# A routed-expert encoder block on one core: down sums in groups of 128 columns, weight slots returned one by one, and filler products on TensorE

## The chip, the cores and the metric

The kernel runs on one core of one Trainium2 chip. The metric is the device time of one execution in microseconds, shown as the median of several runs. The names of the engines are those of the profile: PE is TensorE (PEld its weight loads), DVE is VectorE, ACT is ScalarE, POOL is GpSimd, SP is SyncE, which here only issues DMA transfers.

## What is computed

One layer of an encoder on 256 tokens of 2,048 channels, all in float32. The reference, cut to what matters here:

```
mod = silu(c) @ W_ada + b_ada                     # 2048 x 12288: shift, scale, gate, twice
h   = rmsnorm(x, g_pre_mix) * (1 + sc1) + sh1
y   = hybrid_mixer(h, ...)                        # w_in (2048 x 10752), two branches, w_branch_a/b, w_out
x   = x + gt1 * rmsnorm(y, g_post_mix)
h   = rmsnorm(x, g_pre_ffn) * (1 + sc2) + sh2
aff = softmax(h @ w_router)                       # 256 tokens x 16 experts
top_aff, top_idx = top_k(aff.T, 32)               # each expert picks its 32 tokens
for each expert e:                                # FF = 1024
    xe = h[top_idx[e]]
    ye = (silu(xe @ w_gate[e]) * (xe @ w_up[e])) @ w_down[e]
    y[top_idx[e]] += top_aff[e] * ye
x   = x + gt2 * rmsnorm(y, g_post_ffn)
```

## The kernel before

**Tiles and slots.** Every weight matrix is laid out ahead of time as tiles of 128 partitions x 2,048 float32, 1 MB each, and read once from HBM: 96 tiles of `w_ada`, 84 of `w_in`, 8 + 8 of the branch projections, 16 of `w_out`, and for each of the 16 experts 16 tiles of gate and up columns (`w_gu`) and 8 of the down matrix (`w_dn`). SBUF has 27 slots of that size (`Mem`, a first-in first-out list). `take()` (lines 155 to 163) gets a slot and issues one transfer on SP's queue; if the slot is still being read by an engine, SP waits there, and all later transfers behind it. The order of the tiles, `stream`, is fixed ahead: first the mixer's program `prog` (lines 231 to 272), then expert after expert.

**The mixer.** Each tile of a projection is split into a high and a low part (`split`, lines 427 to 440: ACT copies at line 436, DVE subtracts at line 437), and `prod` (lines 442 to 466) does three TensorE products for each pair of parts. The parts live in a ring of `NHL = 6` of the 27 slots (`Ring`, lines 107 to 123), which come back to the common list only when the mixer's program is through (`hring.close()`, line 896). The merged branch results, MH and ML, take two slots each (each of them holds two of the four k-steps of the last projection); they too are returned at the very end (line 856). A `w_ada` tile ("A", "B" items) is no TensorE work but one DVE instruction (line 402). The constants in lines 35 to 38 say how many such tiles are mixed in where: BL for the late `w_in` projections (30 items with 12 tiles, then 14 with 14), BD for the branch projections and the last projection (16 items with 8 tiles, then the 14 of 16 that follow with 14).

**From the mixer to the first expert** (lines 899 to 1047). DVE and ACT finish the normalised residual X2 (`rsqrt`, lines 217 to 228, is a logarithm and an exponential on ACT with a Newton step on DVE). TensorE turns X2 and multiplies it by the router's matrix, a softmax follows, TensorE turns the affinities (line 967), DVE selects the 32 largest of each expert in four rounds (lines 971 to 981), TensorE turns the marks back (line 984), and `gather_first` (lines 1014 to 1046) builds the first expert's inputs in four groups of 128 columns: `rows(i)` gathers with one-hot products, `turn_rows(i)` turns them and DVE scales them. Two groups are gathered ahead of the first expert tile.

**The experts** (lines 1063 to 1163). For each of the 16 tiles k, four products go to four column strips of the array (`tile_position=(0, 32 * j)`), 512 columns each; then the tile's slot is returned. After the sixteenth, SiLU and the product `he`. The down matrix is done in four chunks of 512 output columns: `down_wide` (line 1141) sums two tiles into four strips that each hold a part of the contraction, and `combine_wide` (line 1152) has two TensorE products with `stw` (the affinities at the tokens' places, repeated for the four strips), which add the strips and scatter to 2 x 128 tokens; DVE adds the result to ACC (line 1160).

**The last expert and the output** (lines 1165 to 1228). Here the down matrix goes by nine steps (`STEPS`: seven of 256 columns, two of 128, the last tile in two transfers): `down(i)`, `combine(i - 1)`, then `squares(i - 2)` for the final norm (ACT; DVE for the last two), and `gain3(i - 2)`, the product with the post-norm gain on DVE (one step on GpSimd). Then the squares are reduced (line 1209), `rsqrt` with two late `gain3` in its shadow, and the output is formed and stored.

The order on an engine is that of the program text, unless `after(engine, f)` pins an instruction to come behind the latest one of its engine; on DVE, the whole order of the last expert is pinned from `mark` on (`finish_deps`). The lines of the order around the change:

```
STEPS = [(256 * i, 256) for i in range(7)] + [(1792, 128), (1920, 128)]   # line 35
BL = [(30, 12), (14, 14)]                                                # 37
BD = [(16, 8), (14, 14)]                                                 # 38
hring.put(hl)                                                            # 466, at the end of prod
if c == 3: mem.put(*MH, *ML)                                             # 855-856, only at q == 3
rows(0); rows(1); turn_rows(0)                                           # 1036-1038
```

## Time and profile before

| what | value |
|---|---|
| median of three runs | 1692.03 us (1691.38 to 1692.73) |
| the profiled execution | 1690.94 us, its span 1689.2 us |
| instructions | 19531 |
| mean granted TensorE clock | 0.911 of full speed |
| busy: PE, DVE, ACT, POOL | 1412.3, 769.1, 544.5, 1.6 us |
| HBM read, mean rate over the span | 630.04 MB, 374 GB/s |

Times in the trace count from the start of the span, in microseconds. The ends of matmuls are modelled, so a busy PE is not PE at its peak; a share of busy time is an average over stages that have different limits, so it has to be read stage by stage. A row of the timeline gives start, busy time, engine, line of the kernel, operation, output and inputs, how many instructions it stands for, and in brackets how long the engine had been idle before it and on what. The profile counts a float32 product as two instructions, each with its own weight load.

### The profile page before, as it was taken

To read this page: it belongs to the slowest core of one execution; us is meant where nothing else is said; L and a number is where in the kernel's file an instruction comes from. 1 tells how busy PE (TensorE), PEld (TensorE's weight loads), DVE (VectorE), ACT (ScalarE), POOL (GpSimd) and SP (SyncE) were. 2 spreads that over 40 slices of the span, in tenths; PEclk is the share of its full clock that TensorE was granted. 3 is DMA by queue.
4 is the path that set the end of the run, shared out by engine and by line. 5 is a ranking of instruction groups with operands and counts; after the bars stand their busy time and mean duration, and the time that the engine had idled before them with its cause. 6 is when DMAs were issued, how large, how long until landed. Compare 5 with 4: busy or idle time off the path is not lost.

```text
span 1689.2 us, 19531 instructions
## 1 busy us (share of the span) xinstructions
PE 1412.3 (84%) x7982; PEld 787.6 (47%) x7982; DVE 769.1 (46%) x1017; ACT 544.5 (32%) x793; POOL 1.6 (0%) x5
## 2 busy tenths in 40 slices
PE   4999999999999999988877776776776677677677
PEld 3999997787888888862211111111111111111113
DVE  8788879989878799742111111110111111111013
ACT  6577777765575434431100000000000000000013
POOL 0000000000000000000000000000000000000000
PEclk7999999999999999998998888797878979788798
DMA  9999975665778879989999999999999999999996
GB/s 386 420 421 375 356 324 223 254 233 198 293 277 341 348 280 377 421 355 420 421 421 420 421 421 421 421 420 421 421 422 421 421 422 421 421 421 421 422 421 279
DMA packets 88505, 633.41 MB, mean 375 GB/s; under 512 B 10080, under 2 KB 10464, under 8 KB 11744
## 3 DMA queue, kind: packets, MB, share of 16 engines
q1 hardware_dynamic: 88128, 631.39, 91.8%
q8 instruction: 62, 1.02, 0.2%
q10 hardware_dynamic: 288, 0.79, 0.1%
q14 instruction: 27, 0.22, 0.0%
HBM read 630.04 MB, written 2.10 MB: 374 GB/s over the span
## 4 chain that ended last, share of the span: by engine, by line
PE 48%; DMA 45%; DVE 3%; ACT 2%; issue 1%; SPq 0%; ACTq 0%; DVEq 0%
PE PS L180 46%; DMA w<-in_w_gu_dram 32%; DMA w<-in_w_dn_dram 12%; DMA w<-in_w_in_dram 1%; DVE hl L437 1%; DMA w<-in_w_ada_dram 1%; ACT ew L1150 0%; DVE w L402 0%; PE PS L917 0%; PE PS L1092 0%; PE PS L688 0%; DVE F L510 0%; ACT hl L436 0%; ACT ew L1089 0%; PE PS L770 0%
## 5 line engine op out<-in xcount | busy, mean ns | idle before, releaser
L180 PE MATMUL PS<-w,rt 128*32 128x512 f32 x2048 | 336.2, 727 | 155.8 <-DMA w<-in_w_gu_dram 154.9
L437 DVE TENSOR_TENSOR hl<-w,hl 128x1024 fp32r<-128x1024 f32 x232 | 278.0, 1220 | 87.2 <-ACT hl L436 86.4
L180 PE MATMUL PS<-hl,hl 128*128 128x256 f32 (+1 forms) x928 | 309.1, 334 | 0.0
L436 ACT CAST hl<-w 128x1024 fp32r<-128x1024 f32 x232 | 237.8, 1048 | 151.7 <-PE PS L180 142.9
L180 PE MATMUL PS<-hl,hh 128*128 128x512 f32 x832 | 269.8, 399 | 0.7 <-ACT hl L436 0.6
L180 PEld LDWEIGHTS PS<-w,rt 128*32 128x32 f32 x2048 | 52.3, 117 | 388.8 <-DMA w<-in_w_gu_dram 338.7
L402 DVE SCALAR_TENSOR_TENSOR w<-w,crow 128x2048 f32<-128x2048 f32 x96 | 218.8, 2284 | 3.7 <-DMA w<-in_w_ada_dram 3.5
L180 PE MATMUL PS<-hh,hl 128*128 128x256 f32 x1024 | 186.7, 285 | 9.3 <-ACT hh L420 9.3
L180 PEld LDWEIGHTS PS<-hl,hl 128*128 128x128 f32 x928 | 177.5, 191 | 16.3 <-issue 1.0
L1160 DVE TENSOR_TENSOR acc<-acc,PS 128x1024 f32<-128x1024 f32 x56 | 68.4, 1221 | 244.3 <-PE PS L180 244.3
L180 PE MATMUL PS<-ew,rt 128*128 128x512 f32 (+2 forms) x276 | 138.9, 629 | 45.1 <-ACT ew L1150 45.1
L180 PEld LDWEIGHTS PS<-hl,hh 128*128 128x128 f32 x832 | 155.4, 188 | 33.5 <-ACT hl L436 1.0
L180 PEld LDWEIGHTS PS<-hh,hl 128*128 128x128 f32 x1024 | 161.5, 194 | 9.6 <-ACT hh L420 9.5
L180 PE MATMUL PS<-w,ew 128*32 128x512 f32 (+2 forms) x1104 | 145.9, 636 | 19.7 <-DVE ew L1098 15.4
L1098 DVE TENSOR_TENSOR ew<-ew,PS 128x256 f32<-128x256 f32 x16 | 6.7, 421 | 241.0 <-ACT ew L1097 241.0
L180 PEld LDWEIGHTS PS<-ew,rt 128*128 128x128 f32 x276 | 49.4, 200 | 141.0 <-ACT ew L1150 105.6
L1150 ACT COPY ew<-PS 128x512 f32<-128x512 f32 x60 | 35.1, 585 | 237.1 <-PE PS L180 237.1
L1089 ACT COPY ew<-PS 128x512 f32<-128x512 f32 x16 | 9.4, 585 | 237.1 <-PE PS L180 237.1
L180 PEld LDWEIGHTS PS<-w,ew 128*32 128x32 f32 x1104 | 29.0, 118 | 118.5 <-issue 68.9
L180 PE MATMUL PS<-hl,mh 128*128 128x512 f32 x256 | 80.1, 393 | 0.0
L1053 DVE TENSOR_SCALAR rt<-ct,rt 128x128 f32<-128x128 f32 x32 | 9.6, 343 | 147.6 <-PE PS L1057 147.6
L1059 ACT COPY rt<-PS 128x256 f32<-128x256 f32 x16 | 6.0, 372 | 191.5 <-PE PS L1057 191.5
(252 smaller groups left out, 1111.1 us busy)
## 6 DMA issues: line engine op xcount, KB each, us to landing
w<-in_w_gu_dram SPq DMA_DIRECT2D x256, 1024.0 KB, 19.8
w<-in_w_dn_dram SPq DMA_DIRECT2D x127, 1024.0 KB, 19.8
w<-in_w_ada_dram SPq DMA_DIRECT2D x96, 1024.0 KB, 8.9
w<-in_w_in_dram SPq DMA_DIRECT2D x84, 1024.0 KB, 7.2
w<-in_w_out_dram SPq DMA_DIRECT2D x16, 1024.0 KB, 14.7
w<-in_w_a_dram SPq DMA_DIRECT2D x8, 1024.0 KB, 6.8
w<-in_w_b_dram SPq DMA_DIRECT2D x8, 1024.0 KB, 8.2
x<-in_x_dram SPq DMA_DIRECT2D x4, 1024.0 KB, 12.2
```

The source lines that it names most:

```text
L180: E.matmul(o, l, r, start=start, stop=stop, skip_group_check=True, **kw)
L402: V.scalar_tensor_tensor(t, t, 1.0, CR, ALU.mult, ALU.mult, accum_out=MOD[:, p, k:k + 1])
L436: S.copy(hl[:, 0, :], w)
L437: V.tensor_tensor(hl[:, 1, :], w, hl[:, 0, :].bitcast(F32), ALU.subtract)
L1053: V.tensor_scalar(rp[:, tt], io[:, None, :].to_broadcast([128, 4, 32]), pm3[:, tt, e:e + 1], aff[:, tt, e:e + 1], ALU.is_equal, ALU.mult)
L1059: S.copy(stw, b[:, :256])
L1089: S.copy(gu, b)
L1098: V.tensor_tensor(he, sl_, b3[:, :, 64:128], ALU.mult)
L1150: S.copy(EW[:, 2, :], b)
L1160: V.tensor_tensor(a, a, p3, ALU.add)
```

## The change

It has five parts.

1. **Slots and order of the mixer.** `Ring.put` gets the number of parts still to come (`todo`) and hands a slot back to the common list as soon as the ring's free slots are enough for them. MH and ML are returned in halves, at the second and the fourth k-step of the last projection. Four `w_ada` tiles are moved from the last projection to earlier ones: two to the late `w_in` projections, two to the branch projections.
2. **Fillers.** `warm(n, ...)` issues n float32 products of the identity with itself, whose result nobody reads: 11 behind the mixer's last product, 6 behind the router's sums, 20 behind the turn of the affinities.
3. **The path to the first expert.** `rsqrt` may be one ACT function (`Abs_reciprocal_sqrt`), used for the mixer's and the final norm; the squares of the residual are placed otherwise between ACT and DVE; the softmax works on both halves at once; `gather_first` gathers one group, not two, ahead of the first tile, and goes on with one half step between tiles.
4. **Down sums.** In all experts each chunk of 512 columns is done in four groups of 128: `down_quarters` puts group j, over the whole contraction, into strip j (16 products of 128 columns a tile), and `combine_quarters` scatters it with products of 32 rows (`tile_position=(32 * j, 0)`), eight a chunk, of 128 columns. ACT's copy has 128 columns, not 512. The combination of chunk c - 1 stands behind the products of chunk c.
5. **The last expert.** Three chunks of 512, then one step of 256 and two of 128. The gain of chunk 2 is half on GpSimd, half on DVE, that of the 256 columns on GpSimd; the layout of the last expert's tiles follows.

```diff
-STEPS = [(256 * i, 256) for i in range(7)] + [(1792, 128), (1920, 128)]
+WIDE = [(512 * i, 512) for i in range(4)]
+STEPS = WIDE[:3] + [(1536, 256), (1792, 128), (1920, 128)]
 BE = [2, 2, 2, 10]
-BL = [(30, 12), (14, 14)]
-BD = [(16, 8), (14, 14)]
+BL = [(30, 14), (14, 14)]
+BD = [(16, 10), (14, 10)]
...
-    def put(self, t):
-        self.slots.append(self.mem.slot.pop(id(t))[0])
+    def put(self, t, todo):
+
+        if todo <= len(self.slots):
+            self.mem.put(t)
+        else:
+            self.slots.append(self.mem.slot.pop(id(t))[0])
...
+        if direct:
+            S.activation(r, ss, AF.Abs_reciprocal_sqrt, scale=1.0 / D, bias=epsc)
+        else:
+            S.activation(l, ss, AF.Ln, scale=1.0 / D, bias=epsc)
+            S.activation(r, l, AF.Exp, scale=-0.5)
...
+    nsplit = [sum(it[0] in ("W", "YA", "YB", "O") for it in prog)]
...
-            hring.put(hl)
+            hring.put(hl, 2 * nsplit[0])
...
-                if c == 3:
-                    mem.put(*MH, *ML)
+            if c == 3 and q % 2:
+                mem.put(MH[q // 2], ML[q // 2])
...
+    def warm(n, o):
+
+        for _ in range(n):
+            after(mybir.EngineType.PE, lambda: mm(o, ident, ident, True, True))
+
+    warm(11, PS[:, 3072:3200])
...
+    warm(6, PS[:, 0:128])
     rm, rd = tiny(2), tiny(2)
     V.tensor_reduce(rm, l3, AX.X, ALU.max)
-    V.tensor_scalar(rm, rm, -1.0, None, ALU.mult)
+    V.tensor_tensor(l3, l3, rm[:, :, None].to_broadcast([128, NT, 16]), ALU.subtract)
...
+    warm(20, PS[:, 0:128])
...
         rows(0)
-        rows(1)
         turn_rows(0)
         yield xe
         for i in range(1, 4):
-            if i < 3:
-                after(mybir.EngineType.PE, lambda: rows(i + 1))
+            after(mybir.EngineType.PE, lambda: rows(i))
+            yield
             after(mybir.EngineType.PE, lambda: turn_rows(i))
             yield
...
+        def down_quarters(i):
+
+            b = bank()
+            for h in range(2):
+                w = take()
+                for kq in range(4):
+                    for j in range(4):
+                        mm(b[32 * j:32 * j + 32, :128], he[:, kq, 32 * h:32 * h + 32],
+                           w[:, 512 * kq + 128 * j:512 * kq + 128 * j + 128], h == 0 and kq == 0,
+                           h == 1 and kq == 3, tile_position=(0, 32 * j))
+                mem.put(w)
+            S.copy(sums(i), b[:, :128])
+
+        def combine_quarters(i):
+
+            ps = PS[:, :2048].rearrange("p (j r t c) -> p t j r c", j=4, r=2, t=2)[:, :, :, i % 2, :]
+            for tt in range(NT):
+                for j in range(4):
+                    mm(ps[:, tt, j, :], stw[32 * j:32 * j + 32, 128 * tt:128 * tt + 128],
+                       sums(i)[32 * j:32 * j + 32, :], True, True, tile_position=(32 * j, 0))
+            a = acc(i).rearrange("p t (j c) -> p t j c", j=4)
...
+                V.tensor_tensor(a, a, ps, ALU.add)
...
-            for c in range(4):
-                down_wide(c)
-                combine_wide(c)
+            for c in range(5):
+                if c < 4:
+                    down_quarters(c)
+                if c:
+                    after(mybir.EngineType.PE, lambda: combine_quarters(c - 1))
             continue
...
+        for i in range(3):
+            down_quarters(i)
+            if i:
                 after(mybir.EngineType.PE, lambda: combine(i - 1))
-            if 1 < i < ns:
-                squares(i - 2)
-                if i < ns - 1:
-                    gain3(i - 2)
-        gain3(ns - 3, nc.gpsimd)
-        squares(ns - 1)
+                squares(i - 1)
+                gain3(i - 1)
+        w = take()
+        after(mybir.EngineType.PE, lambda: combine(2))
+        after(mybir.EngineType.PE, lambda: down(3, w))
+        mem.put(w)
+        squares(2)
+        gain3(2, nc.gpsimd, slice(0, 1))
+        gain3(2, V, slice(1, 2))
...
+        squares(5)
+
+        nc.gpsimd.tensor_copy(tiny(1), sf8[:, 1, 5:6])
+        after(mybir.EngineType.Pool, lambda: gain3(3, nc.gpsimd))
...
-    r3 = rsqrt(sf, 2, lambda: (gain3(7), gain3(8)))
+    r3 = rsqrt(sf, 2, lambda: (gain3(4), gain3(5)), True)
```

The first place in the order is TensorE's between the router and the first tiles of the first expert (ct: the sum over strips of the router's products; rt: router's scratch; ident: turns and fillers; x: the residual, gathered from; w: expert tiles; line 180 is the common product helper, 185 after the change). Before:

```order
L180 MATMUL PS<-ct,rt_5864 128x16 x2
L967 MATMUL PS<-ident,rt_5864 16x128 x2
L984 MATMUL PS<-ident,rt_5864 128x16 x2
L180 MATMUL PS<-x_726_5593,rt_5864 32x128 x4
L180 MATMUL PS<-x_727_5595,rt_5864 32x128 x4
L180 MATMUL PS<-x_726_5593,rt_5864 32x128 x4
L180 MATMUL PS<-x_727_5595,rt_5864 32x128 x4
L1031 MATMUL PS<-ident,rt_5864 128x128
L180 MATMUL PS<-w_5996,rt_5864 32x512 x4
L180 MATMUL PS<-x_726_5593,rt_5864 32x128 x4
L180 MATMUL PS<-x_727_5595,rt_5864 32x128 x4
```

With the change:

```order
L185 MATMUL PS<-ct,rt_5875 128x16 x2
L185 MATMUL PS<-ident 128x128 x6
L988 MATMUL PS<-ident,rt_5875 16x128 x2
L185 MATMUL PS<-ident 128x128 x20
L1006 MATMUL PS<-ident,rt_5875 128x16 x2
L185 MATMUL PS<-x_728_5596,rt_5875 32x128 x4
L185 MATMUL PS<-x_729_5598,rt_5875 32x128 x4
L1053 MATMUL PS<-ident,rt_5875 128x128
L185 MATMUL PS<-w_6023,rt_5875 32x512 x4
L185 MATMUL PS<-x_728_5596,rt_5875 32x128 x4
L185 MATMUL PS<-x_729_5598,rt_5875 32x128 x4
L185 MATMUL PS<-w_6038,rt_5875 32x512 x4
```

Six and twenty fillers stand between, one gather group (eight rows of x as two times four) stands ahead of the first tile and not two, and each turn comes a tile later than its group.

The second place is TensorE's order in the last expert, to the last products with the sums, before from behind the fifth of the nine steps on, with the change from behind the fourth down tile on (w: down tiles, the last one in two halves; ew: the sums and `he`; rt: holds `stw`). Before:

```order
L180 MATMUL PS<-ew_6059,rt_5864 128x256 x2
L180 MATMUL PS<-w_9061,ew_6059 32x256 x8
L180 MATMUL PS<-ew_6059,rt_5864 128x256 x2
L180 MATMUL PS<-w_9078,ew_6059 32x256 x8
L180 MATMUL PS<-ew_6059,rt_5864 128x256 x2
L180 MATMUL PS<-w_9095,ew_6059 32x128 x8
L180 MATMUL PS<-ew_6059,rt_5864 128x256 x2
L180 MATMUL PS<-w_9095,ew_6059 32x128 x8
L180 MATMUL PS<-ew_6059,rt_5864 128x128 x4
```

With the change:

```order
L185 MATMUL PS<-ew_6095,rt_5875 128x128 x3
L185 MATMUL PS<-w_10911,ew_6095 32x128 x16
L185 MATMUL PS<-ew_6095,rt_5875 128x128 x5
L185 MATMUL PS<-w_10929,ew_6095 32x128 x16
L185 MATMUL PS<-ew_6095,rt_5875 128x128 x10
L185 MATMUL PS<-w_10960,ew_6095 32x256 x8
L185 MATMUL PS<-w_10984,ew_6095 32x128 x8
L185 MATMUL PS<-ew_6095,rt_5875 128x256 x2
L185 MATMUL PS<-w_10984,ew_6095 32x128 x8
L185 MATMUL PS<-ew_6095,rt_5875 128x128 x4
```

Nine steps of which each is followed by the combination of the one before it have become three chunks and three small steps; in these rows the sixth down tile is the fourth one, the combination of chunk 1 stands around it, and that of chunk 2 behind it.

The third place is VectorE's order there (acc: the sums over all experts, in two halves; G: the gain; line 1209, after the change 1248, is the reduction of the squares). Before:

```order
L1126 TENSOR_TENSOR acc_6150<-acc_6150,PS 128x2x256
L1139 TENSOR_TENSOR acc_6149<-acc_6149,G_1487_8861 128x2x256
L1126 TENSOR_TENSOR acc_6150<-acc_6150,PS 128x2x256
L1139 TENSOR_TENSOR acc_6150<-acc_6150,G_1487_8861 128x2x256
L1126 TENSOR_TENSOR acc_6150<-acc_6150,PS 128x2x256
L1139 TENSOR_TENSOR acc_6150<-acc_6150,G_1487_8861 128x2x256
L1126 TENSOR_TENSOR acc_6150<-acc_6150,PS 128x2x128
L1133 SCALAR_TENSOR_TENSOR rt_5864,small<-acc_6150 128x128
L1126 TENSOR_TENSOR acc_6150<-acc_6150,PS 128x2x128
L1133 SCALAR_TENSOR_TENSOR rt_5864,small<-acc_6150 128x128
L1209 TENSOR_REDUCE small<-small 128x2
```

With the change:

```order
L1161 TENSOR_TENSOR acc_6185<-acc_6185,PS 128x2x512
L1194 TENSOR_TENSOR acc_6185<-acc_6185,G_1493_10701 128x2x512
L1161 TENSOR_TENSOR acc_6185<-acc_6185,PS 128x2x512
L1194 TENSOR_TENSOR acc_6185<-acc_6185,G_1493_10701 128x2x512
L1161 TENSOR_TENSOR acc_6186<-acc_6186,PS 128x2x512
L1194 TENSOR_TENSOR acc_6186<-acc_6186,G_1493_10701 128x512
L1179 TENSOR_TENSOR acc_6186<-acc_6186,PS 128x2x256
L1179 TENSOR_TENSOR acc_6186<-acc_6186,PS 128x2x128
L1187 SCALAR_TENSOR_TENSOR rt_5875,small<-acc_6186 128x128
L1179 TENSOR_TENSOR acc_6186<-acc_6186,PS 128x2x128
L1187 SCALAR_TENSOR_TENSOR rt_5875,small<-acc_6186 128x128
L1248 TENSOR_REDUCE small<-small 128x2
```

The adds (lines 1126; 1161 and 1179) and the gain products (1139; 1194) alternate in both; those of 256 columns have become ones of 512, and the gain of half of chunk 2 stands between its add and the add of the 256 columns.

## Rows read from the trace of the kernel before

**Rows 1.** The page, the chain of work that ended last: shares of the span by engine.

```profile
PE 48%; DMA 45%; DVE 3%; ACT 2%; issue 1%; SPq 0%; ACTq 0%; DVEq 0%
```

**Rows 2.** Windows over the span: start and end in us, length; busy us and count of PE, PEld, DVE, ACT, POOL; granted TensorE clock, share of the DMA engines, GB/s.

```profile
300.00:400.00 100.00, 98.79 (x519) 80.04 (x518) 92.38 (x136) 65.32 (x90) 0.00 (x0) 1.00 0.55 205
...
600.00:650.00 50.00, 50.00 (x231) 41.56 (x231) 48.56 (x54) 20.50 (x22) 0.00 (x0) 1.00 0.84 326
...
750.00:800.00 50.00, 37.81 (x319) 14.34 (x312) 17.50 (x60) 11.57 (x28) 0.00 (x0) 0.86 1.01 420
...
1600.00:1650.00 50.00, 38.40 (x198) 8.77 (x190) 6.27 (x6) 5.06 (x9) 0.00 (x0) 0.87 1.01 421
```

**Rows 3.** The timeline of SP's queue from 735 to 800 us: start, length, and the number of transfers issued in the row.

```profile
742.76 1.28 SPq L161 DMA_DIRECT2D w<-in_w_gu_dram  x3
744.08 10.72 SPq L161 DMA_DIRECT2D w<-in_w_dn_dram  x8
769.61 27.97 SPq L161 DMA_DIRECT2D w<-in_w_gu_dram  x16
```

**Rows 4.** Windows of 2 us, with the columns of group 2.

```profile
740.00:742.00 2.00, 2.00 (x11) 1.65 (x10) 0.00 (x0) 0.00 (x0) 0.00 (x0) 1.00 0.00 0
...
760.00:762.00 2.00, 0.00 (x0) 0.00 (x0) 1.86 (x7) 0.00 (x0) 0.00 (x0) 0.50 1.00 418
...
768.00:770.00 2.00, 2.00 (x24) 0.79 (x16) 0.00 (x0) 0.00 (x0) 0.00 (x0) 0.50 1.00 418
```

**Rows 5.** Transfers issued in three narrow windows: from 742.7 to 742.9 us (the issue of 742.76), from 754.4 to 754.6 (the last of the eight down tiles, at 754.47) and from 769.5 to 769.8 (the one at 769.61). The last number is the time from issue to landing in us.

```profile
w<-in_w_gu_dram SPq DMA_DIRECT2D x1, 1024.0 KB, 4.7
...
w<-in_w_dn_dram SPq DMA_DIRECT2D x1, 1024.0 KB, 19.2
...
w<-in_w_gu_dram SPq DMA_DIRECT2D x1, 1024.0 KB, 6.6
```

**Rows 6.** The timeline from the mixer's last product to the third tile of the first expert.

```profile
742.34 0.39 PE L180 MATMUL PS<-hl,mh 128*128 128x512 f32 x1
...
743.66 0.68 DVE L854 TENSOR_TENSOR yg<-PS,yg 128x512 f32<-128x512 f32 x1
...
757.57 0.59 PE L967 MATMUL PS<-ident,rt 128*16 128x128 f32 x2 [2.08 <-DVE rt L964]
758.20 0.42 DVE L972 MAX8 rt<-PS 16x8 f32<-16x256 f32 x1 [0.55 <-PE PS L967]
...
763.54 0.39 PE L984 MATMUL PS<-ident,rt 16*128 16x16 f32 x2 [5.38 <-DVE rt L981]
...
764.55 1.94 PE L180 MATMUL PS<-x,rt 128*32 128x128 f32 x32 [0.62 <-DVE rt L993]
...
767.61 1.94 PE L180 MATMUL PS<-w,rt 128*32 128x512 f32 x8 [0.71 <-DVE rt L1034]
...
770.33 0.33 PE L1031 MATMUL PS<-ident,rt 128*128 128x128 f32 x1
...
771.47 0.62 PE L180 MATMUL PS<-x,rt 128*32 128x128 f32 x16
...
772.28 1.07 PE L180 MATMUL PS<-w,rt 128*32 128x512 f32 x8
```

**Rows 7.** The timeline of the last expert's down steps and what follows them.

```profile
1668.77 1.07 PE L180 MATMUL PS<-w,ew 128*32 128x256 f32 x16
...
1674.62 0.64 PE L180 MATMUL PS<-w,ew 128*32 128x128 f32 x16
...
1675.20 1.22 PE L180 MATMUL PS<-ew,rt 128*128 128x128 f32 x8
1675.34 0.68 DVE L1139 TENSOR_TENSOR acc<-acc,G 128x512 f32<-128x512 f32 x1
...
1676.26 2.74 PE L180 MATMUL PS<-x,ident 128*128 128x512 f32 x6
...
1676.49 0.29 DVE L1133 SCALAR_TENSOR_TENSOR rt<-acc 128x128 f32<-128x128 f32 x1
1676.54 1.37 POOL L1139 TENSOR_TENSOR acc<-acc,G 128x512 f32<-128x512 f32 x1 [1676.10 <-ACT rt L1135]
...
1677.16 0.90 DVE L1133 SCALAR_TENSOR_TENSOR rt<-acc 128x128 f32<-128x128 f32 x1
...
1678.17 0.17 DVE L1209 TENSOR_REDUCE small<-small 128x2 f32<-128x18 f32 x1
...
1678.45 0.75 DVE L1139 TENSOR_TENSOR acc<-acc,G 128x256 f32<-128x256 f32 x2
```

**Rows 8.** Groups of instructions over the whole span, forms kept apart: line, engine, operation, operands and count, then busy time in us, mean ns of one, and idle time before with what ended it.

```profile
L180 PE MATMUL PS<-w,rt 128*32 128x512 f32 x2048 | 336.2, 727 | 155.8 <-DMA w<-in_w_gu_dram 154.9 <-DVE rt L1034 0.7
...
L402 DVE SCALAR_TENSOR_TENSOR w<-w,crow 128x2048 f32<-128x2048 f32 x96 | 218.8, 2284 | 3.7 <-DMA w<-in_w_ada_dram 3.5
...
L1160 DVE TENSOR_TENSOR acc<-acc,PS 128x1024 f32<-128x1024 f32 x56 | 68.4, 1221 | 244.3 <-PE PS L180 244.3
...
L929 ACT ACTIVATE rt<-x 128x512 f32<-128x512 f32 x4 | 2.5, 636 | 1.4 <-DVE x L912 1.4
```

**Rows 9.** The page, DMA queues of the instruction fetch: packets, MB, share of the 16 engines.

```profile
q8 instruction: 62, 1.02, 0.2%
...
q14 instruction: 27, 0.22, 0.0%
```

More of the change, by code (lines that the diff above doesn't have):

```diff
@@ L937, in block_kernel @@
         after(mybir.EngineType.PE, lambda: logits(c - 1))
-        if c > 1:
-            after(mybir.EngineType.DVE, lambda: res_squares(c - 2))
+        res_squares(c - 1, True)
     logits(3)
-    res_squares(2)
-    res_squares(3)
+    res_squares(3, True)
+    for c in range(4):
+        after(mybir.EngineType.DVE, lambda: res_squares(c, False))
     V.tensor_reduce(sx, sq8.rearrange("p (t c) -> p t c", t=2), AX.X, ALU.add)
@@ L1078, in block_kernel @@
             mem.put(w)
-            if e == 0 and k < 3:
+            if e == 0 and k < 6:
                 next(first)
@@ L1122, in combine @@
         def combine(i):
+            if i < 3:
+                return combine_quarters(i)
             ps, n = cbank(), STEPS[i][1]
@@ L1169, in block_kernel @@
-        ns = len(STEPS)
-        for i in range(ns + 1):
-            if i < 7:
-                w = take()
-                down(i, w)
-                mem.put(w)
-            elif i == 7:
-                w, t = mem.get([D], F32, "w"), stream[cursor[0]]
-                cursor[0] += 1
-                for h in range(2):
-                    nc.sync.dma_start(w[:, 1024 * h:1024 * h + 1024], t[:, 1024 * h:1024 * h + 1024])
-                down(7, w[:, :1024])
-            elif i == 8:
-                down(8, w[:, 1024:])
-                mem.put(w)
-            if i == ns:
-                squares(i - 2)
-            if i > 0:
-                after(mybir.EngineType.PE, lambda: combine(i - 1))
-            if 1 < i < ns:
-                squares(i - 2)
-                if i < ns - 1:
-                    gain3(i - 2)
@@ new lines, in block_kernel @@
+        w = take()
[5 more added lines that the diff above has]
+        gain3(2, V, slice(1, 2))
+        w, t = mem.get([D], F32, "w"), stream[cursor[0]]
+        cursor[0] += 1
+        for h in range(2):
+            nc.sync.dma_start(w[:, 1024 * h:1024 * h + 1024], t[:, 1024 * h:1024 * h + 1024])
+        after(mybir.EngineType.PE, lambda: down(4, w[:, :1024]))
@@ L1199, in blk @@
+        after(mybir.EngineType.PE, lambda: combine(3))
+        squares(3)
+        after(mybir.EngineType.PE, lambda: down(5, w[:, 1024:]))
+        mem.put(w)
+        after(mybir.EngineType.PE, lambda: combine(4))
+        squares(4)
+        after(mybir.EngineType.PE, lambda: combine(5))
+        squares(5)
+        nc.gpsimd.tensor_copy(tiny(1), sf8[:, 1, 5:6])
+        after(mybir.EngineType.Pool, lambda: gain3(3, nc.gpsimd))
     def blk(c):
```

77 lines of the change are left out of this document (35 added, 42 removed).

## The prediction, made before the changed kernel was run

> **What bounds the kernel now.** I read the chain of waits first. It is split between TensorE and DMA, nearly half each [rows 1]. The wide windows show where each rules [rows 2]: from 750 us on the DMA engines run at 1.01 of their share and 420 GB/s, while TensorE is busy 38.40 of 50 us in a stretch in the middle of the experts. There a product saved is worth nothing: time is gained only by starting this stream earlier, by putting less into it, or by shortening what follows its last byte. Before 750 us it is the other way round: TensorE is busy 50.00 of 50 us from 600 us on, and its work there is not touched.
>
> The stream starts late for a reason that the queue of SyncE shows [rows 3]: with 13 expert tiles issued, nothing follows in this window until 742.76 us, when the mixer's last product ends (742.73 [rows 6]) and slots come free; three tiles and the eight down tiles follow, and then nothing until 769.61 us. By then 24 tiles fill all slots that the experts have (27 less the residual pair and the router's tile), and the 25th must wait until TensorE has read the first. Narrow windows show what the first hole costs [rows 4]: 0 GB/s at 740 us. The landings show the second [rows 5]: the 25th tile, issued at 769.61, lands 6.6 us later, at 776.2, only 2.5 us behind the 24th, issued at 754.47, which lands at 773.7. So the second wait is hidden in the old kernel, by 2 us or so. A tile issued to an empty queue (742.76) takes 4.7 us.
>
> **The change, part by part.**
>
> *Slots returned singly; half the merged tiles returned at the second of four steps; four ada tiles moved out of the last projection.* These fill the first hole, some 6.6 us of transfer. But no slot is added: 24 tiles can be loaded before the router is through, not one more. The last two of them still wait for the router's own tiles, near 754 us, so the 24th lands at about 754.5 + 1 + 4.7 + 2.5 = 762.7 us, and then DMA stands still until the first expert tile is read. The whole gain therefore depends on when that is.
>
> *The path to the first expert tile.* In the trace that tile's read ends at 769.55: 767.61 plus 1.94 [rows 6]. After TensorE has idled, the clock granted is 0.50 at 760 and at 768 us, i.e. 1.2 of 2.4 GHz [rows 4]. The fillers (11, 6 and 20 products of 128 columns) keep TensorE at work there. At full clock 16 gather instructions take 0.62 us and an expert tile 1.07; at half clock 32 took 1.94 and a tile 1.94 [rows 6]. Only one gather group, not two, now stands ahead of the first tile. So from 764.55: gather 0.64 + 0.1, copy 0.3, turn 0.33 + 0.1, two VectorE products 0.7, tile 1.07, in all 3.3 with the handovers, against 5.0: 1.7 saved. Softmax has fewer steps (0.2) and two earlier turns run at full clock (0.4): 2.3 saved. The direct root saves nothing: VectorE is then still at its last product of the mixer [rows 6], and in the tail at two gain products [rows 7]. Against it: the 20 fillers stand between the turn at 757.57 and the one at 763.54. Four such products, 8 instructions, took 1.22 us, and 1.06 from their start to that of the next work [rows 7], so 20 take 5.3 to 6.1; VectorE's selection, from 758.20 to the turn at 763.54 [rows 6], takes 5.3. I charge 0.2; between 0 and 0.8.
>
> *The ada tiles.* Two more come in the late projections and two more in the branch projections, each 2.28 us of VectorE [rows 8]. VectorE is busy 92.38 of 100 us in the first and 48.56 of 50 in the second [rows 2], and TensorE needs its splits. Nothing to 4.6 us for either; I take 1 us on the mixer's end, since TensorE shows 1.2 us of idle time in the first and none in the second.
>
> So the first release comes at 769.6 - 2.3 + 0.2 + 1.0 = 768.5, the 25th tile lands 4.7 later, at 773.2, instead of 776.2. Gain 3.0, less the thinner queue of a single tile in flight: I take **-2.7** (0 to -6.6; the ends are no gain, and the first hole filled with no second).
>
> *Down sums by 128 columns.* Per expert, 32 products become 128 and 8 combining products become 32, the latter of a quarter of the rows. Per tile, TensorE's 8 instructions of 1.07 us [rows 6] become 32 of 0.04 (16 took 0.64 [rows 7]), 1.28 us. A combination of four row groups has no row: side by side like the column groups it takes 0.64, one after the other, by the row of 8 instructions of 128 columns in 1.22, its 16 take 2.4 [rows 7]. Either way TensorE stays far under the stream's pace, so it is hidden. What is not hidden is the code: 1,800 more products in 15 experts are four instructions each in the profile (a load and a product, twice: the 1,024 products of the experts' first half stand as 2,048, and as many loads [rows 8]). The two instruction queues fetched 1.24 MB [rows 9] for the page's 19531 instructions, 64 bytes each; 7,200 more are 0.46 MB in a stream that is full: at 420 GB/s **+1.1** (0 to 2, the latter by the share of the engines that the queue takes in the profile).
>
> *The tail.* Old: TensorE is the pace, eight combinations behind nine steps, and the reduction of the squares starts at 1678.17 [rows 7]. New: three wide steps, and VectorE has the pace, since its order is written down: it may not add chunk 2 before it has multiplied chunk 1 by the gain, which waits for both squares of chunk 1. From the sixth down tile, at TensorE by 1668.5: products 1.28 and the last two combining ones 0.2, so 1670.0. Sum 1.22, squares 2 x 0.72 (0.636 and what its read-out adds), gain 1.22, next sum 1.22 [rows 8]: 1675.1. Squares of chunk 2: first done at 1675.9, second 1676.6. GpSimd then multiplies half of chunk 2 for 1.37 us, until 1677.3, while VectorE is to multiply the other half. Next to GpSimd's one product in the old tail a VectorE product of two tiles in SBUF took 0.90 instead of 0.29 us, ending 0.15 after GpSimd's did [rows 7]. So I let VectorE wait until 1677.3: half product 0.68, sum 0.69 (512 elements either, as the gain product at 1675.34 [rows 7]), squares of 256 columns 0.8, then two small squares and one small sum 1.2: reduction at 1680.8. After it GpSimd's second product again runs beside two gain products of VectorE, which held 0.75 us in the old kernel: another 1.3. Tail **+4.0** (+1.9 if nothing waits for GpSimd; 0 to +5).
>
> The Trainium skill says, in SBUF — State Buffer, on the shared port pair, that a VectorE instruction with two SBUF inputs and a GpSimd one that reads SBUF exclude each other for a whole instruction. By that rule both places wait in full, the +4.0 above; by the single row's loss of 0.6 at each it would be +3.1.
>
> The sum is -2.7 + 1.1 + 4.0 = +2.4. On the profiled execution, 1690.94 us, that is 1693.3; this execution lies 1.1 under the median of the runs, 1692.03, so I forecast 1694.4.
>
> **The rivals.** *A, slower: the ada tiles make VectorE the bound of the mixer.* If the 4.6 us of either place come through to the mixer's end, every release behind it is as much later. For it: 48.56 of 50. Against: TensorE idles nowhere there, and the splits run two items ahead. Decides at more than 1.4 us of VectorE work per 50 us. 1694.4 + 3.6 = 1698.0.
>
> *B, faster: the first tile is read much earlier, or the tail does not wait.* If the clock and the shorter path bring the release to 766 us (gain 5), and VectorE and GpSimd do not collide (tail +1.9), with code fetched in gaps: 1692.03 - 5 + 1.9 = 1688.9; with the old tail's length kept, 1687.0. For it: the 0.50 clock from 760 to 770 us. Against: the order on VectorE.
>
> *C, TensorE becomes the bound of the experts*, since its combinations now wait for VectorE's sum before (1.2 us, three times an expert) and it changes between column and row groups some eleven times. It decides when TensorE needs over 59.7 us per expert (24 tiles); in the middle stretch it needed 38.40 of 50, i.e. 46. Products save 4 x 1.1 and cost 8 x 0.2, waits 3.7: near 47. If 1 us of each change were lost, 58. Price if over by 1: +15, 1709. The Trainium skill says, in TensorEngine Tiling (Array Packing), Key Properties, that a change of tiling mode drains TensorE; no row shows that alone.
>
> *D, the change does nothing that can be told*: gain and costs cancel; that is my forecast's own middle.
>
> **How the numbers follow.** About 0.2%, 3.4 us, can be told from no change; so faster is under 1688.6, slower over 1695.4. Forecast 0.56, A 0.19, B 0.20, C 0.05. Faster: B's lower part and a little of the forecast's, 0.22. Slower: A, C and the forecast's upper end, 0.31. Same 0.47. Range 1686.5 to 1698.5: B's lower end to just over A.
>
> **What would show it.** Right: DMA unbroken from 690 to about 763 us, then a hole of some 7 us, then the first tile read near 768.5; clock 1.0 there; steady 420 GB/s after; instruction queues at some 1.7 MB; VectorE's half product and gain products stretched to GpSimd's end; and the reduction 4 us later, measured from the last down tile. Wrong: no hole at 763; a mixer that ends over 2 us off 743.7; or a tail no longer than now.

## The result: slower by 12.5 us, outside the range

The changed kernel took 1704.33 us (median of 4, 1700.44 to 1704.92) against 1691.78 us of the kernel before (1691.38 to 1692.73); the ratio is 1.0069, 95% interval 1.0057 to 1.0082. The forecast was 1694.4, the range 1686.5 to 1698.5. It is slower by over 0.2%, the case to which the prediction gave 0.31.

The profiled execution has a span of 1702.6 us against 1689.2, 13.4 more. The page after, against [rows 1, 9]: span, TensorE's instruction queue (number of packets, MB, share), shares of the chain of work that ended last.

```profile
span 1702.6 us, 27098 instructions
...
q8 instruction: 92, 1.51, 0.4%
...
PE 48%; DMA 44%; DVE 5%; ACT 1%; issue 1%; SPq 0%; ACTq 0%; DVEq 0%
```

The chain is split nearly as before, but 30 more packets of code were fetched. The 2 us windows around the first expert tile, against [rows 4]:

```profile
740.00:742.00 2.00, 2.00 (x11) 1.65 (x10) 0.00 (x0) 0.00 (x0) 0.00 (x0) 1.00 1.05 446
...
760.00:762.00 2.00, 2.00 (x20) 2.00 (x20) 1.86 (x7) 0.00 (x0) 0.00 (x0) 1.00 1.00 418
...
766.00:768.00 2.00, 0.99 (x5) 0.32 (x9) 0.93 (x4) 0.24 (x1) 0.00 (x0) 0.86 0.00 0
768.00:770.00 2.00, 2.00 (x28) 1.21 (x24) 0.00 (x0) 0.00 (x0) 0.00 (x0) 0.50 0.03 8
```

The first hole is gone (446 GB/s at 740 us, 0 before), a second one is there (0 at 766 us), and the clock stays at 1.0 until 766 us, then falls to 0.50 just as the first tile is read (TensorE was busy for 0.99 us of the 2.00 before). The queue of SyncE, against [rows 3]:

```profile
736.49 19.03 SPq L166 DMA_DIRECT2D w<-in_w_dn_dram  x8
769.28 25.74 SPq L166 DMA_DIRECT2D w<-in_w_gu_dram  x16
```

All eight down tiles are issued by 755.5 us, and the 25th tile at 769.28, instead of 769.61 before. In the next rows, of the transfers: the time from issue to landing of the 25th tile (issued at 769.28), of two tiles issued at 860.4 and 862.9 us, and the code packets in the windows from 884 to 1006 and from 1006.5 to 1134.8 us.

```profile
w<-in_w_gu_dram SPq DMA_DIRECT2D x1, 1024.0 KB, 4.8
...
w<-in_w_dn_dram SPq DMA_DIRECT2D x1, 1024.0 KB, 19.8
...
w<-in_w_dn_dram SPq DMA_DIRECT2D x1, 1024.0 KB, 20.8
...
q8 instruction: 8, 0.13, 0.4%
...
q8 instruction: 8, 0.13, 0.4%
```

The 25th tile lands at 774.09, 2.1 us earlier than before. Then the lead is lost. By the 38th tile it is 0.8 us (landings at 807.88 and 808.63), and then it turns into a delay: in a stream that is otherwise nearly even, the time from issue to landing steps from 19.8 to 20.8 us, and such steps of about 1 us come at 785, 884, 1007, 1135, 1264, 1392, 1518 and 1659 us, with eight code packets between two of them. Before there were three (959, 1222 and 1482), the same eight packets apart. The last tile lands at 1678.71 (issue at 1661.06 plus 17.65), 5.3 us later than before (1673.40): from the 25th landing to the last the stream takes 904.6 us, not 897.2. Of these 7.4 us 1.3 are lost up to the 38th tile, and 6.1 behind it.

The path to the first tile, against [rows 6]:

```profile
744.23 0.39 PE L185 MATMUL PS<-hl,mh 128*128 128x512 f32 x1
...
758.81 4.63 PE L185 MATMUL PS<-ident 128*128 128x128 f32 x40
...
764.35 0.29 PE L1006 MATMUL PS<-ident,rt 16*128 16x16 f32 x2 [0.91 <-DVE rt L1003]
...
765.27 0.64 PE L185 MATMUL PS<-x,rt 128*32 128x128 f32 x16 [0.62 <-DVE rt L1015]
...
767.34 1.90 PE L185 MATMUL PS<-w,rt 128*32 128x512 f32 x8 [0.71 <-DVE rt L1056]
```

The mixer ends at 744.62, not 742.73; from there to the end of the first tile's read (769.24) it takes 24.6 us, not 26.8. The last expert, against [rows 7]: TensorE and VectorE from the fourth down tile on, then GpSimd and the reduction.

```profile
1672.06 0.71 PE L185 MATMUL PS<-ew,rt 32*128 32x128 f32 x4
...
1672.80 1.22 DVE L1161 TENSOR_TENSOR acc<-acc,PS 128x1024 f32<-128x1024 f32 x1 [9.57 <-PE PS L185]
...
1674.17 0.46 PE L185 MATMUL PS<-ew,rt 32*128 32x128 f32 x2 [1.41 <-DVE acc L1161]
...
1674.56 1.21 PE L185 MATMUL PS<-w,ew 128*32 128x128 f32 x32
...
1675.69 1.22 PE L185 MATMUL PS<-ew,rt 32*128 32x128 f32 x10
...
1676.84 1.94 PE L185 MATMUL PS<-w,ew 128*32 128x128 f32 x32
...
1678.71 0.73 PE L185 MATMUL PS<-ew,rt 32*128 32x128 f32 x4
...
1679.47 1.22 DVE L1161 TENSOR_TENSOR acc<-acc,PS 128x1024 f32<-128x1024 f32 x1 [2.68 <-PE PS L185]
...
1680.84 0.73 PE L185 MATMUL PS<-ew,rt 32*128 32x128 f32 x16 [1.41 <-DVE acc L1161]
...
1682.30 1.22 DVE L1194 TENSOR_TENSOR acc<-acc,G 128x1024 f32<-128x1024 f32 x1 [1.60 <-ACT rt L1189]
...
1683.44 1.21 DVE L1161 TENSOR_TENSOR acc<-acc,PS 128x1024 f32<-128x1024 f32 x1
...
1685.55 1.26 POOL L1194 TENSOR_TENSOR acc<-acc,G 128x512 f32<-128x512 f32 x1 [1685.11 <-ACT rt L1189]
...
1686.26 1.11 DVE L1194 TENSOR_TENSOR acc<-acc,G 128x512 f32<-128x512 f32 x1 [1.60 <-ACT rt L1189]
...
1690.74 0.17 DVE L1248 TENSOR_REDUCE small<-small 128x2 f32<-128x12 f32 x1 [0.20 <-ACT rt L1189]
1690.75 1.26 POOL L1194 TENSOR_TENSOR acc<-acc,G 128x512 f32<-128x512 f32 x1
1690.94 1.09 DVE L230 TENSOR_SCALAR small<-small 128x2 f32<-128x2 f32 x1
```

The sixth tile landed at 1673.45, by the trace, and is read at 1676.84, 3.4 us later, and at half the clock: 1.94 us for 32 instructions that take 1.08 in the run pinned below. Ahead of it TensorE's order has a single combining product of chunk 1 (1674.17), which waited for VectorE's add of chunk 0 (1672.80 to 1674.02) while the fifth tile, there since 1670.97, waited behind it; five more products of chunk 1 (1675.69) stand between the fifth tile and the sixth. The reduction stands at 1690.74, 12.0 us behind the last landing, not 4.8; from it to the end it takes 11.8, not 11.0. So of the 13.4 us the start gave -2.1, the stream +7.4 and the tail +8.1. Of the run old_order below, the one execution with a trace took 1941.21 us at a mean granted clock of 0.726, so its trace isn't used.

### The profile page after: what moved, and what is told of

It is laid out like the page before. It is cut to its first block, busy times and chain, and to the rows that moved or that the text cites. A ratio compares the mean times of both kernels' runs of the same rounds, so it can differ in the third digit from the quotient of the medians.

```text
span 1702.6 us, 27098 instructions
## 1 busy us (share of the span) xinstructions
PE 1428.0 (84%) x11776; PEld 955.3 (56%) x11776; DVE 768.7 (45%) x1011; ACT 524.5 (31%) x778; POOL 2.9 (0%) x7
## 3 DMA queue, kind: packets, MB, share of 16 engines
q8 instruction: 92, 1.51, 0.4%
## 4 chain that ended last, share of the span: by engine, by line
PE 48%; DMA 44%; DVE 5%; ACT 1%; issue 1%; SPq 0%; ACTq 0%; DVEq 0%
PE PS L185 47%; DMA w<-in_w_gu_dram 30%; DMA w<-in_w_dn_dram 13%; DMA w<-in_w_in_dram 1%; DVE acc L1161 1%; DVE hl L447 1%; DMA w<-in_w_ada_dram 1%; DVE w L410 0%; DVE x L931 0%; PE PS L699 0%; PE PS L1113 0%; PE PS L781 0%; DVE F L521 0%; DVE T L535 0%; DVE T L525 0%
## 5 line engine op out<-in xcount | busy, mean ns | idle before, releaser
L185 PE MATMUL PS<-w,rt 128*32 128x512 f32 x2048 | 327.3, 721 | 132.6 <-DMA w<-in_w_gu_dram 131.7
L185 PEld LDWEIGHTS PS<-w,rt 128*32 128x32 f32 x2048 | 58.7, 121 | 343.8 <-DMA w<-in_w_gu_dram 262.4
L185 PE MATMUL PS<-w,ew 128*32 128x128 f32 (+1 forms) x4080 | 187.4, 348 | 27.4 <-DVE ew L1119 15.4
L185 PE MATMUL PS<-ew,rt 32*128 32x128 f32 (+1 forms) x1020 | 120.7, 370 | 66.1 <-DVE acc L1161 59.5
L185 PEld LDWEIGHTS PS<-w,ew 128*32 128x32 f32 x4080 | 143.5, 140 | 57.9 <-DVE ew L1119 20.5
L185 PEld LDWEIGHTS PS<-ew,rt 32*128 32x128 f32 (+1 forms) x1020 | 88.9, 243 | 105.9 <-issue 88.1
L1147 ACT COPY ew<-PS 128x128 f32<-128x128 f32 x63 | 16.7, 265 | 309.3 <-PE PS L185 307.2
L1110 ACT COPY ew<-PS 128x512 f32<-128x512 f32 x16 | 9.4, 585 | 234.2 <-PE PS L185 234.2
L185 PEld LDWEIGHTS PS<-hl,mh 128*128 128x128 f32 x256 | 48.1, 188 | 10.9 <-issue 1.0
L1015 DVE TENSOR_SCALAR rt<-ct,rt,small 128x32 f32<-128x32 f32 x32 | 9.3, 300 | 98.9 <-PE PS L185 98.9
## 6 DMA issues: line engine op xcount, KB each, us to landing
w<-in_w_dn_dram SPq DMA_DIRECT2D x127, 1024.0 KB, 19.8
```

The source lines that it names most:

```text
L185: E.matmul(o, l, r, start=start, stop=stop, skip_group_check=True, **kw)
L1015: V.tensor_scalar(oh[:, tt, :], io, pm3[:, tt, e:e + 1], r2[:, tt:tt + 1], ALU.is_equal, ALU.mult)
L1110: S.copy(gu, b)
L1147: S.copy(sums(i), b[:, :128])
```

## The experiments

All times are beside runs of the kernel before on the same chip, 1691.6 to 1691.7 us.

**1. Code without the rest of the change.**

```diff
             b = bank()
+            for _ in range(30):
+                mm(b[:32, :16], ident[:, :32], ident[:, :16], True, True)
             for h in range(2):
                 w = take()
```

> The kernel before, with 1,800 products added that nobody reads: 30 of 32 by 16 ahead of each chunk of down sums in 15 experts, into a bank that the next product overwrites. They are the number of products that the change adds there, with nothing else of the change. Theory 1 (the stream is longer because TensorE's instructions are fetched in packets of 16 KB through the same DMA engines, about 1.05 us of one engine each, in turn over eight engines): 28 more packets, the time from the 25th tile's landing to the last grows from 897 us by 4 to 7.5 us, and the run takes 4 to 7.5 us more than the kernel before. Rival 1 (it is the new order of the combining products and their waits on VectorE that releases slots late): no more than 1 us. My forecast's term: 1.1 us.

1697.80 us, ratio 1.0036 (1.0023 to 1.0049): 6.2 more. The stream takes 903.2 us, 6.0 more than before. **2. TensorE's time without the code**, the same place with another loop:

```diff
+            for _ in range(3):
+                mm(b[:32, :], ident[:, :32], X2[0][:, :512], True, True)
```

> The kernel before, with TensorE's time of the run code_alone and a tenth of its code: 3 products of 32 by 512 that nobody reads, not 30 of 32 by 16, ahead of each chunk of down sums in 15 experts, some 2.7 us a chunk against some 2.4. Theory 1 (packets of code): 3 more packets, within 1 us of the kernel before. Rival 1 (TensorE's additional time, and with it the later release of slots, makes the stream longer): as code_alone, 6 us more than before.

1692.84 us, ratio 1.0006 (0.9997 to 1.0015): 1.1 more, a hair over the 1 us that theory 1 allowed; the stream takes 898.4 us. The first two rows are from the pages, TensorE's busy time with the code and with the time; it was 1412.3 us before. The next ones are the code packets between the 25th and the last landing, with the code, with the time, and in the kernel before:

```profile
PE 1493.6 (88%) x11582; PEld 923.5 (54%) x11582; DVE 769.4 (45%) x1017; ACT 545.4 (32%) x793; POOL 1.6 (0%) x5
...
PE 1489.3 (88%) x8342; PEld 829.4 (49%) x8342; DVE 769.3 (45%) x1017; ACT 544.7 (32%) x793; POOL 1.6 (0%) x5
```

```profile
q8 instruction: 58, 0.95, 0.4%
```

```profile
q8 instruction: 32, 0.52, 0.2%
```

```profile
q8 instruction: 30, 0.49, 0.2%
```

The changed kernel has 58, as the run with the code. 28 packets more cost 6.0 us of stream, nearly the same time on TensorE with 2 packets more 1.2. So it is the code, not the time and not the order of the combinations. The traces of all runs that can be compared agree: from the 38th landing to the last, the six executions with 54 to 56 code packets there (the change, code_alone, old_tail, pinned, gain_late, no_gpsimd) take 870.3 to 870.9 us, the six with 28 (the kernel before, old_down, front_only, no_fillers, slots_only, dense) 864.5 to 864.9.

**3. The two halves undone one at a time.** Old down sums in 15 experts:

```diff
...
-            for c in range(5):
-                if c < 4:
-                    down_quarters(c)
-                if c:
-                    after(mybir.EngineType.PE, lambda: combine_quarters(c - 1))
+            for c in range(4):
+                down_wide(c)
+                combine_wide(c)
```

> The changed kernel, with the down sums and combinations of the first 15 experts as before (chunks of 512 columns in four strips, two combining products), and everything else as changed. Theory 1 (code in the stream): packets of TensorE's code fall from 92 to about 63, the stream from the 25th tile to the last is again about 897 us, and the run is 5 to 7.5 us faster than the changed kernel's 1704.3, 1697 to 1699. Rival 2 (the later end is the tail's alone, and the late last tile a consequence of a slower start): 1704.

1697.11 us (ratio to the kernel before 1.0031, 1.0020 to 1.0041), 7.2 less than the change; the stream takes 898.7 us with 30 code packets, 5.9 less, and what follows the last landing 22.7 us, 1.1 less. The old last expert instead:

```diff
-STEPS = WIDE[:3] + [(1536, 256), (1792, 128), (1920, 128)]
+STEPS = [(256 * i, 256) for i in range(7)] + [(1792, 128), (1920, 128)]
...
+        for i in range(ns + 1):
+            if i < 7:
+                w = take()
+                down(i, w)
+                mem.put(w)
...
```

> The changed kernel, with the last expert's nine steps and their layout as before; the first 15 experts, the fillers and the slots stay as changed. Theory 2 (the last expert's order costs 8.1 us from the last landing to the end): the reduction of the squares comes 4.8 us after the last landing, not 12.0, and the run takes 7 to 8 us less than 1704.3, 1696 to 1697.5. My forecast's term was 4.0 us: 1700.3.

1697.07 us (1.0032, 1.0020 to 1.0044), 7.3 less; the reduction comes 5.5 us after the last landing. Both together, the front of the change alone:

> The changed kernel with both the first 15 experts' down sums and the last expert's nine steps as before: of the change only the slots, the order of the w_ada tiles, the fillers, the softmax, the first gather and the direct root stay. If the two losses measured apart (7.2 us in the 15 experts, 7.3 us in the last one) are independent, 1704.3 - 14.5 = 1689.8 us, 1.9 us less than the kernel before, with the 25th tile's landing at 774.0 against 776.2. If they are not, over 1692.

1690.08 us (0.9992, 0.9984 to 1.0001): the two losses add up, within 0.3 us. The gain over the kernel before can't be told from none, though the 25th tile lands 1.8 us earlier (774.38).

**4. The order in the last expert.** First every combining product pinned:

```diff
-                    mm(ps[:, tt, j, :], stw[32 * j:32 * j + 32, 128 * tt:128 * tt + 128],
+                    after(mybir.EngineType.PE, lambda: mm(
+                        ps[:, tt, j, :], stw[32 * j:32 * j + 32, 128 * tt:128 * tt + 128],
...
```

> The changed kernel, with each of the eight combining products of a chunk pinned behind the one before it, not only the first: no single product of a combination can be placed ahead of a later down tile. Theory 3 (TensorE reads the sixth down tile of the last expert 3.4 us after its landing because one combining product, placed ahead of the fifth tile, waits for VectorE's add of the chunk before): the sixth tile is read within 0.5 us of its landing, and the run takes 2 to 3.5 us less than 1704.3, 1700.8 to 1702.3. Rival (VectorE's own chain of add, gain and add is the pace, whenever the sixth tile is read): within 1 us of 1704.3.

1700.40 us (1.0052, 1.0040 to 1.0065), 3.9 less than the change, somewhat more than expected. The edit pins the combinations of all experts, but the stream stays as it was (905.2 us). The timeline from the sixth tile on, which landed at 1673.93:

```profile
1673.97 1.08 PE L185 MATMUL PS<-w,ew 128*32 128x128 f32 x32 [1.40 <-DMA w<-in_w_dn_dram]
...
1674.98 0.73 PE L185 MATMUL PS<-ew,rt 32*128 32x128 f32 x16
...
1675.78 1.22 DVE L1162 TENSOR_TENSOR acc<-acc,PS 128x1024 f32<-128x1024 f32 x1 [0.98 <-PE PS L185]
...
1677.14 0.73 PE L185 MATMUL PS<-ew,rt 32*128 32x128 f32 x16 [1.43 <-DVE acc L1162]
...
1678.60 1.23 DVE L1195 TENSOR_TENSOR acc<-acc,G 128x1024 f32<-128x1024 f32 x1 [1.60 <-ACT rt L1190]
...
1679.74 1.21 DVE L1162 TENSOR_TENSOR acc<-acc,PS 128x1024 f32<-128x1024 f32 x1
```

It is read at once, and the reduction comes 7.7 us behind the last landing, not 12.0: about 3.4 of these 4.4 us are the earlier read. Part of the rest goes with the clock, which stays at 1.0 here from 1667.8 us to the reduction and was 0.50 in the change from 1675.4 to 1678.8 us and from 1682.2 to 1689.0; no run separates the two. What is left shows in the last three rows: the add of chunk 2 (1679.74) stands behind the gain of chunk 1 (1678.60), though its products are through at 1677.87. Placing that gain behind the add:

```diff
-                gain3(i - 1)
+                if i < 2:
+                    gain3(i - 1)
         w = take()
         after(mybir.EngineType.PE, lambda: combine(2))
+        gain3(1)
```

> The changed kernel with all combining products pinned (as in the run pinned), and in the last expert the gain product of chunk 1 on VectorE placed behind the add of chunk 2, not ahead of it. Theory 6 (what remains of the last expert's loss is VectorE's written order: the add of chunk 2 waits for the squares and the gain of chunk 1, though its input is there 1.8 us earlier): 1.4 to 1.8 us less than pinned, 1698.6 to 1699.0, and the reduction 5.9 to 6.3 us after the last landing instead of 7.7. Rival (ScalarE's squares of chunk 1 and chunk 2 one after the other are the pace): no gain over 0.5 us.

1698.43 us (1.0043, 1.0029 to 1.0057): 2.0 less than pinned, the reduction 6.0 us behind the last landing. Theories 3 and 6 hold, with gains 0.2 to 0.4 us above what was expected. Then GpSimd's two products given to VectorE:

```diff
-        gain3(2, nc.gpsimd, slice(0, 1))
-        gain3(2, V, slice(1, 2))
+        gain3(2)
...
-    r3 = rsqrt(sf, 2, lambda: (gain3(4), gain3(5)), True)
+    r3 = rsqrt(sf, 2, lambda: (gain3(3), gain3(4), gain3(5)), True)
```

> The kernel gain_late, with both gain products that GpSimd has in the last expert given to VectorE. Theory 9 (VectorE's half gain, 1.11 us and not 0.68, and the first small step of the root, 1.09 us and not 0.17, last until GpSimd's product beside them ends): the whole gain of chunk 2 takes 1.22 us, the small step 0.17 us, and the time is within 0.5 us of gain_late's 1698.4, since VectorE gets 1.2 us of products and loses 1.35 us of waiting. Rival (both are long for another reason): the small step stays at 1.09 us.

1698.47 us (1.0042, 1.0028 to 1.0056), as gain_late. The whole gain of chunk 2, and the small step ahead of the root, which was 1.09 us in the change:

```profile
1681.01 1.22 DVE L1195 TENSOR_TENSOR acc<-acc,G 128x1024 f32<-128x1024 f32 x1 [1.05 <-ACT rt L1190]
...
1685.37 0.17 DVE L230 TENSOR_SCALAR small<-small 128x2 f32<-128x2 f32 x1
```

So VectorE did wait for GpSimd in the change: its small step began at 1690.94 and ended at 1692.03, GpSimd's product at 1692.01.

**5. The start.** The front of the change without its fillers:

```diff
-    warm(11, PS[:, 3072:3200])
...
-    warm(6, PS[:, 0:128])
...
-    warm(20, PS[:, 0:128])
```

> The same as the kernel with the front of the change only, without the 37 filler products. Theory 4 (the fillers keep the granted clock at 1.0 from the mixer's end to 766 us, which makes the turns and the gather ahead of the first tile cheaper by 0.8 to 1.5 us): 0.8 to 1.5 us slower than with them, the clock at 748 and 760 us near 0.5 again. Rival (TensorE waits for VectorE and ScalarE there, whatever its clock, and the first tile itself is still read at 0.5): no difference over 0.3 us.

1693.38 us (1.0010, 1.0001 to 1.0019), 3.3 slower than with them, over twice the upper end of what was expected. Windows at two places, and the read of the first tile:

```profile
750.00:752.00 2.00, 2.00 (x11) 2.00 (x10) 2.00 (x5) 1.57 (x3) 0.00 (x0) 0.50 1.01 422
...
764.00:766.00 2.00, 0.00 (x0) 0.00 (x0) 1.86 (x7) 0.00 (x0) 0.00 (x0) 0.50 0.87 360
```

```profile
771.38 1.93 PE L185 MATMUL PS<-w,rt 128*32 128x512 f32 x8 [0.71 <-DVE rt L1053]
```

From the mixer's end (745.78) to the first tile's end it takes 27.5 us, with the fillers 23.9, and before the change 26.8. Of the 3.6 us between the two, 2.1 lie ahead of the turn of the affinities and 1.4 behind the turn of the marks. The clock was 0.50 from 748.3 to 755.1 us and again from 761.9 on. The slots alone, in the kernel before (`Ring.put`, and MH and ML in halves):

> The kernel before, with the slots of the ring and of the merged branch results returned one by one as in the change, and nothing else. Theory 7 (24 tiles are all that fits; the first hole is filled, and a second one opens ahead of the 25th, which waits for the first tile's read at 769.6 us): the 24th tile lands near 767.5 and not 773.7, the 25th near 774.4 and not 776.2, and the run takes 1 to 2 us less than before. Rival (every tile that comes earlier is time saved): 6 us less.

1691.81 us (1.0001, 0.9992 to 1.0010): nothing. The 24th tile landed at 770.76, the 25th at 775.09, 1.1 us earlier than before. Neither theory's time came out, and the windows behind the second hole show where the lead goes:

```profile
774.00:776.00 2.00, 2.00 (x21) 0.69 (x21) 0.58 (x2) 0.00 (x0) 0.00 (x0) 1.00 1.04 360
776.00:778.00 2.00, 2.00 (x22) 0.62 (x18) 0.61 (x2) 0.37 (x1) 0.00 (x0) 1.00 0.89 307
778.00:780.00 2.00, 2.00 (x26) 0.53 (x18) 0.00 (x0) 0.00 (x0) 0.00 (x0) 1.00 0.94 385
```

The stream starts again at 360, 307 and 385 GB/s, and 420 only then; the 26th tile lands at 779.74, later than the 778.94 of the kernel before. The DMA engines are busy in these windows (shares of 1.04, 0.89 and 0.94), so a lack of issued tiles doesn't explain it alone. The changed kernel loses its time there otherwise:

```profile
772.00:774.00 2.00, 2.00 (x33) 0.83 (x25) 0.29 (x1) 0.27 (x1) 0.00 (x0) 1.00 1.05 434
```

It is at 434 GB/s in the second window behind its hole, and then a step of 1 us comes between the 28th landing and the 29th (781.81 and 785.26). What is common is the sum: from the 25th landing to the 38th, the three kernels that return the slots as before (before, code_alone, time_alone) take 32.3 to 32.5 us, and those with the early return 33.8 to 35.0. So 1.3 to 2.6 us of what the earlier release gains are lost in these thirteen tiles. Why the tiles behind an empty queue come slower isn't settled.

Last, the w_ada tiles placed as before, and then more fillers with them:

```diff
-BL = [(30, 14), (14, 14)]
-BD = [(16, 10), (14, 10)]
+BL = [(30, 12), (14, 14)]
+BD = [(16, 8), (14, 14)]
```

> The same as the kernel with the front of the change only, with the w_ada tiles placed as before (12 and 8 ahead of the last projection, 14 in it). Theory 5 (the four tiles moved forward make the mixer end 1.9 us later): the mixer's last product ends near 742.7 us and not 744.6, the first tile is read 1.9 us earlier, and the run takes up to 1.9 us less. Rival (the four tiles in the last projection keep the slots of expert tiles, and the stream is held up ahead of the 24th tile instead): no gain, or a loss of up to 2 us.

1689.56 us (0.9986, 0.9977 to 0.9995), 0.5 less than the front alone.

```diff
-    warm(20, PS[:, 0:128])
+    warm(24, PS[:, 0:128])
...
+    warm(3, PS[:, 0:128])
     pm = RT[:, 32:64]
...
         rows(0)
+        warm(1, PS[:, 0:128])
         turn_rows(0)
+        warm(3, PS[:, 0:128])
```

> The front of the change with the w_ada tiles placed as before (as in old_order), and more fillers: 24 and not 20 behind the turn of the affinities, 3 ahead of the gather, 1 and 3 around the turn of the first group. Theory 8 (the clock falls to 0.5 between 766 and 770 us because TensorE is idle half of the time from the last filler to the first tile): the first two tiles are read in 1.07 us each, not 1.9, and the run takes 0.3 to 1 us less than old_order's 1689.6. Rival (the first tile is read when VectorE's products are through, and the next tiles come at the pace of the DMA engines): within 0.3 us of 1689.6. Either way the mixer ends near 742.7 us if the four w_ada tiles cost the 1.9 us, and near 744.6 if not.

1689.11 us (0.9985, 0.9976 to 0.9993): the fastest of all, 2.6 less than the kernel before, and 0.5 less than old_order, too little to tell those two apart. The mixer's last product, then the first two tiles:

```profile
742.50 0.39 PE L185 MATMUL PS<-hl,mh 128*128 128x512 f32 x1
...
765.80 1.06 PE L185 MATMUL PS<-w,rt 128*32 128x512 f32 x8
...
767.12 1.04 PE L185 MATMUL PS<-w,rt 128*32 128x512 f32 x8
```

The mixer ends at 742.89, so the four w_ada tiles did cost the changed kernel its 1.7 to 1.9 us (five executions with these tiles as before end the mixer at 742.7 to 743.7, eight with them moved at 744.2 to 746.7); both tiles are read at full clock, and the 25th lands at 771.84, 4.3 us earlier than before. Only 2.6 of it reaches the end: again the first tiles behind the hole come slower, so that at the 38th tile (806.25) the lead is 2.4 us.

## Why the prediction was wrong, point by point

- **What bounds the kernel: right.** The stream bounds the experts also after the change; the 25th tile sets its start.
- **The start: right in sum by luck, wrong in its parts.** Forecast were a release at 768.5 and a landing at 773.2; they came at 769.28 and 774.09. The mixer's end was 1.9 us late, not 1.0 (rival A's mechanism, at less than half its price of 4.6), and the path 2.2 us shorter where 2.1 was forecast. But the split of that 2.1 was wrong: from the start of the gather to the end of the first tile 1.7 us were to be saved, and 1.0 were (765.27 to 769.24, against 764.55 to 769.55); ahead of it 0.4, and 1.2 were. Without the fillers nothing is left of the gain, so it hangs on the clock. And the clock fell once more before the first tile, which the prediction had at 1.07 us and the trace at 1.90. The 24th tile landed at 766.69, not 762.7: it was issued at 755.2 behind tiles still under way, the 21st of which landed at 759.24. And the term for what is lost behind the hole, 0.3, was too small: 1.3 here.
- **The code, the first failed step: +1.1 forecast, +6.1 measured.** This is what the stream loses behind the 38th tile, and code_alone loses the same there (870.9 us, not 864.8). The prediction divided 0.46 MB by 420 GB/s, as if code were spread over all 16 engines like a weight tile. The trace has 58 packets of 0.016 MB in the stream, each some 1.0 us of a single engine's time (0.4% of 16 engines for 904.6 us is 58 us). A likely reading, not shown: a tile is through only when its slowest engine is, and with steps of about 1 us at every eighth packet the packets seem to go round eight engines. Which engine took which isn't in the trace, the steps of code_alone are longer (1.4 us), and the smaller steps of about 0.25 us between are not explained. The upper bound, 2, came from the queue's share of the engines, which is again a mean over all 16.
- **The combinations: right that they are hidden in the 15 experts, wrong in the last one.** Rival C named their wait on VectorE, and asked only if TensorE becomes the bound.
- **The tail, the second failed step: +4.0 forecast, +8.1 measured.** The failed sentence is "From the sixth down tile, at TensorE by 1668.5". The order shown ahead of the prediction has 3 and 5 combining products ahead of the fifth and the sixth tile; they were counted, not read: only the first product of a combination is pinned, the others may be placed ahead of a tile, and one of them waited. Pinning took 3.9 us off. The chain on VectorE was forecast rightly (add, squares, gain, add): from the sixth tile's read to the reduction pinned takes 12.6 us, the forecast 12.3. In the change it takes 13.9, with the clock at 0.50 in part of it. That VectorE waits for GpSimd was right too. By the Trainium skill, in SBUF — State Buffer, Who interferes with whom, an instruction of VectorE in a two-port mode and one of GpSimd exclude each other too, the later one waiting for the whole of the other; the trace agrees, a step of two elements in one tensor lasting 1.09 us and not 0.17 beside GpSimd's product, though it doesn't show in which mode the step ran. The prediction expected that wait on the two gain products behind it, and at 1.3 us; it was 0.8.
- **The range** had the code at no more than 2 and the tail at no more than 5; both terms fell outside, on the same side.

## What to carry to other kernels

Where DMA is the bound, instructions are a load on it: count the additional instructions and their packets, and don't price them by their bytes at the rate of all engines. Here a packet of 16 KB cost 0.2 us of a full stream (6.0 us for 28), where its bytes at 420 GB/s are 0.04. A pin on the first instruction of a group doesn't pin the group: read an order row by row for what may wait ahead of the tile on which the end depends. Fillers can pay where TensorE idles ahead of a critical read (3.3 us here); to keep the clock for the read itself they had to reach up to it, though the time that this last step brought can't be told from none. And an earlier start of a stream isn't yet an earlier end: follow the landings on from it.

## What the runs showed that was not expected

- TensorE's code was fetched all through the run, in packets of 16 KB (1.51 MB in 92): 28 packets more made a stream at 420 GB/s some 6 us longer.
- A stream that starts again behind an empty queue lost 1.3 to 2.6 us in its next thirteen tiles; in one run it moved 360, 307 and 385 GB/s in 2 us windows before it was back at 420.
- With the clock at 1.0 instead of 0.50 in most of it, a chain of 27.5 us in which TensorE is busy about half of the time (11.0 of 20 us from 748 to 768) took 3.6 us less.
